# Column-form projections of a float32 encoder trunk: three 256-column products in one half of a bank in place of one 512-column and one 256-column product

## The chip, the cores and the metric

The kernel runs on one core of one Trainium2 chip. The metric is device time in microseconds of one execution; the number that counts is the median of several runs. Lower is better.

## What is computed

The program is a trunk of four post-norm encoder layers over 256 tokens of width 1024 in float32. Every layer is a token mixer followed by a SwiGLU feed-forward part, each with a residual and a layer norm:

```python
for i in range(DEPTH):                      # DEPTH = 4
    kind = i % 3                            # banded attention, GLA, differential attention, banded attention
    y = mixer(h)                            # x @ w_qkv (or w_in) ... @ w_o
    h = layer_norm(DN_ALPHA * h + y)
    h = layer_norm(DN_ALPHA * h + (silu(h @ w_gate) * (h @ w_up)) @ w_down)   # hidden width 2816
```

Nearly all arithmetic lies in the projections: 256 tokens against weight matrices with 1024 or 2816 rows.

## The kernel before

**Two-part float32 products.** TensorE is fed float32r operands. Each float32 operand is split into a high part and a low part, and a product a·w is the sum of three partial products: high·high, high·low and low·high. Activations lie transposed in SBUF as an operand of eight k-tiles `[128, 512]`: columns 0 to 255 are the high parts of the 256 tokens, columns 256 to 511 their low parts. Weights come by DMA on SP's queue in pieces of two k-tiles by 512 columns (`w_tiles`, L99 to L117); ScalarE makes the high part (L110), VectorE the low part (L111).

**Two forms of a projection.** `run_rows` (L141 to L180) puts 128 tokens on the output partitions and 512 weight columns in a bank of PSUM. Its three products, L175, L176 and L177, each load 128 columns of the activations into the array as the stationary operand and stream 512 weight columns. L175 and L176 use the same stationary tile `xh`.

`run_cols` (L182 to L204) puts 128 weight columns on the output partitions and streams the tokens. It works through a chunk of 512 weight columns: four blocks in the order 0, 2, 1, 3, each with eight k-tiles. For one k-tile (a "step" below) L196 streams all 512 columns of the operand, high and low, against the high weights into a whole bank; L197 streams the 256 high columns against the low weights into the first half of the bank. So the bank holds two halves that have to be added, and that is what the `done` callbacks do: ScalarE copies the second half to SBUF and VectorE adds the first half to it.

**Where the column form is used.** The query and key projections of the three attention layers (`qk_done`: four chunks each, L384 to L396), the queries of the GLA layer (`q_done`: one chunk, L729 and L730), and the gate and up projections of the feed-forward part from the third chunk on (`col_done`: nine chunks in each of four layers, L868 to L875). That is 3·4 + 1 + 4·9 = 49 chunks, 49·4·8 = 1568 steps. In the feed-forward part blocks 0 and 1 are gates (Silu, L871), and blocks 2 and 3 are multiplied by them and split into the high and low parts of the hidden operand (`put`, L211 and L212).

**Order of the work.** Each engine runs its instructions in program order. The order is written out by hand: `defer` puts a mixer's follow-up work off by a number of half-steps, and `tick`, called after every second k-tile in the column form, lets it in between the products. PSUM has four banks for projections (`mm`) and four for everything else (`tp`).

**Other products that the prediction uses.** `gate1` of the GLA layer (L667) runs eight products of 256 columns in a row, each with its own 128x128 float32r stationary tile, all into the same 256 columns of one bank. `values2` (L512 to L514) runs three products of 512 columns and then three of 256 columns; L513 and L514 use the same stationary tile `vh`.

Of the kernel before, what the change touches and what calls it, by code (L numbers as in the profile page):

```python
# [12 lines left out]
ALU = mybir.AluOpType  # L13
# [12 lines left out]
RAWB = 6  # weight loads under way, 2 k-tiles each  # L26
WB = 8  # split weights on chip, 2 k-tiles each
LAG = 10  # k-tiles that token half 1 runs behind half 0
# Half-steps of the tensor engine (see run_rows) by which work is put off.
# [6 lines left out]
def trunk_kernel(  # L36
# [63 lines left out]
    # ---------------------------------------------------------------- weights  # L100
    def w_tiles(chunk, s, fine=False):
        """Loads the k-tiles 2s, 2s+1 of a 512-column chunk of the weights and
        returns, per k-tile, their float32r parts (high, low)."""
        raw = wp.tile([P, 2, 512], F32, tag="raw", bufs=RAWB, name=nm("raw"))
        wh = wp.tile([P, 2, 512], F32R, tag="wh", bufs=WB, name=nm("wh"))
        wl = wp.tile([P, 2, 512], F32R, tag="wl", bufs=WB, name=nm("wl"))
        src = chunk[s].rearrange("p (k n) -> p k n", k=2)
        for k in (slice(0, 1), slice(1, 2)) if fine else (slice(0, 2),):
            nc.sync.dma_start(raw[:, k, :], src[:, k, :])
            nc.scalar.copy(out=wh[:, k, :], in_=raw[:, k, :])  # L110
            nc.vector.tensor_tensor(  # L111
                out=wl[:, k, :],
                in0=raw[:, k, :],
                in1=wh[:, k, :].bitcast(F32),
                op=ALU.subtract,
            )
        return [(wh[:, k, :], wl[:, k, :]) for k in range(2)]  # L117

    def late_load(dst, src, seen):
        """A load that is needed late, held back until `seen` is written, to  # L120
        leave the DMA queues to the weights."""
        nc.gpsimd.tensor_copy(dst[:, 0:1], seen)
        nc.gpsimd.dma_start(dst, src)

    # Work of the mixers that follows from a finished product is put off by a
    # number of half-steps (one k-tile of 512 columns for one token half), so
    # that the tensor engine has products to run while its inputs are made.
# [13 lines left out]
    def run_rows(chunks, lag=LAG, order=None, fine=0):  # L141
        """Products in row form (tokens on partitions, 512 columns a bank).
        chunks: (weights, k-tiles, src, done); src(kt) gives the high | low
        k-tile of all tokens, done(t, bank) reads the finished product.
        order lists (token half, chunk, k-tile); without it token half 1 runs
        lag k-tiles behind half 0."""
# [35 lines left out]
    def run_cols(w, src, done):  # L182
        """Products in column form: 128 columns of the weights on partitions,
        all 256 tokens in the free dimension. The bank of a column block holds
        the product with the tokens' high parts | with their low parts (high
        weights only), to be added up."""
        wt = []
        for s in range(NKT // 2):
            wt += w_tiles(w, s)
        for blk in (0, 2, 1, 3):  # L190
            b = bank("mm")
            cs = slice(blk * P, (blk + 1) * P)
            for kt in range(NKT):
                wh, wl = wt[kt]
                xk = src(kt)
                nc.tensor.matmul(b, wh[:, cs], xk, start=kt == 0, stop=False)  # L196
                nc.tensor.matmul(  # L197
                    b[:, :256], wl[:, cs], xk[:, :256], start=False, stop=kt == NKT - 1
                )
                if kt == NKT - 1:  # L200
                    done(blk, b)
                if kt % 2:
                    tick(1)
# [3 lines left out]
    # ------------------------------------------------------------- transposes  # L207
    def put(dst, ks, cs, val):
        """Writes val as the high and low parts of k-tiles ks, tokens cs."""
        h = dst[:, ks, cs]  # L210
        nc.scalar.copy(out=h, in_=val)  # L211
        nc.vector.tensor_tensor(  # L212
            out=dst[:, ks, slice(256 + cs.start, 256 + cs.stop)],
            in0=val,
            in1=h.bitcast(F32),
            op=ALU.subtract,
        )

    def split_T(src_cols, dst, t, k0, n):
        """Transposes n [128,128] blocks (row form in src_cols) into the k-tiles  # L220
        k0.. of token half t of dst."""
        b = bank()
        for k in range(n):
            nc.tensor.transpose(  # L224
                b[:, k * P : (k + 1) * P], src_cols[:, k * P : (k + 1) * P], ident
            )
        put(
            dst,
            slice(k0, k0 + n),
            slice(t * P, (t + 1) * P),  # L230
            b[:, : n * P].rearrange("p (k c) -> p k c", k=n),
        )

    def operand():
        """High | low parts of 8 k-tiles of all tokens."""
        return slab([P, NKT, 4 * P], F32R)
# [4 lines left out]
    # ------------------------------------------------------------- layer norm  # L241
# [12 lines left out]
    class Norm:  # L254
# [12 lines left out]
        def load(self, seen):  # L267
            """The next of the loads that the norm waits for."""
# [63 lines left out]
    def out_proj(OT, w, norm):  # L332
        """The k-tiles that need the last of the mixer's output come late, and
        enough of half 1 after half 0 to cover the norm of half 0."""
# [10 lines left out]
    # ------------------------------------------------- banded softmax attention  # L345
    def attention(xT, wqkv, bias_ap, w_o, norm, diff, src=None, **first):
        """One column block of 128 holds two 64-wide score maps: two heads, or
        the two maps of one differential head."""
# [30 lines left out]
        def qk_done(g):  # L379
            qk = qk_all[:, g, :, :]  # L380

            def done(blk, b):
                lo = k1([P, 256])
                if blk < 2:  # L384
                    nc.scalar.mul(lo, b[:, 256:], 0.125)
                    nc.vector.scalar_tensor_tensor(
                        out=qk[:, blk, :],
                        in0=b[:, :256],
                        scalar=0.125,
                        in1=lo,  # L390
                        op0=ALU.mult,
                        op1=ALU.add,
                    )
                    return
                nc.scalar.copy(out=lo, in_=b[:, 256:])
                nc.vector.tensor_tensor(  # L396
                    out=qk[:, blk, :], in0=b[:, :256], in1=lo, op=ALU.add
                )
# [83 lines left out]
        def turn2(c, pr):  # L482
            """Key block 0: half 0 of both heads, half 1 of both; key block 1:
            half 1 of both heads."""
# [17 lines left out]
        def values2(c, ph, pl):  # L502
            """Values of both heads against the weights of each: the rows of
            the other head are not read."""
# [101 lines left out]
    # ------------------------------------------------- gated linear attention  # L606
    def gla(xT, norm):
# [21 lines left out]
        # Low-rank gate: the columns 0..15 of the stationary tile are the high  # L629
        # parts of w_g1 and 32..47 the low parts (what follows them, the next  # L630
        # k-tile's, gives rows that nothing reads); w_g2 stands in the same
        # rows, so that the second product adds both up, and its bias in row 64.
# [94 lines left out]
        def q_done(blk, b):  # L727
            lo = k1([P, 256])
            nc.scalar.mul(lo, b[:, 256:], HK ** -0.5)  # L729
            nc.vector.scalar_tensor_tensor(  # L730
                out=qT[:, blk, :],
                in0=b[:, :256],
                scalar=HK ** -0.5,
                in1=lo,
                op0=ALU.mult,
                op1=ALU.add,
            )
# [104 lines left out]
    # ----------------------------------------------------------------- swiglu  # L842
    def ffn(xT, layer, norm):
# [19 lines left out]
        def col_done(c):  # L863
            g = {}

            def done(blk, b):
                lo = k1([P, 256])
                nc.scalar.copy(out=lo, in_=b[:, 256:])  # L868
                nc.vector.tensor_tensor(out=lo, in0=b[:, :256], in1=lo, op=ALU.add)  # L869
                if blk < 2:  # L870
                    nc.scalar.activation(lo, lo, AF.Silu)  # L871
# [3 lines left out]
                nc.vector.tensor_tensor(out=lo, in0=lo, in1=gg, op=ALU.mult)  # L875
# [19 lines left out]
    # ------------------------------------------------------------------ trunk  # L895
# [36 lines left out]
def _layouts(inputs):  # L932
    """Weights laid out chunk by chunk as the kernel reads them, x also with
    its tokens last, and the relative-position tables laid out per (query
    partition p, key column c): the key sits c - 128 - p places after the query."""
# [4 lines left out]
    def tiles(w, pairs=0):  # L940
        """[L, K, N] to [L, chunk, K / 256, 128, 2 * 512]; the first `pairs`
        chunks hold 256 columns of each of the first two parts of that width."""
# [68 lines left out]
```

## Time and profile before

| | |
|---|---|
| median of 3 runs | 1212.04 us (1210.23 to 1212.31) |
| span of the profiled execution, first to last instruction | 1209.5 us |
| mean granted TensorE clock, share of full speed | 0.998 |
| instructions | 17080 |
| TensorE matmuls / weight loads | 6224 / 6224 |
| VectorE / ScalarE busy | 829.6 us / 665.5 us |

The profiled execution has no time beside its span; the span is 2.5 us below the median of the runs. The page of the profile lists a matmul's time from its start to the modelled end of its pipeline, so the durations of neighbouring matmuls overlap; the pace of TensorE is read from the distance of their starts. "PEld" is the weight load, which overlaps the matmuls.

### The profile page before, as it was taken

To read this page: it belongs to the slowest core of one execution; us is meant where nothing else is said; L and a number is where in the kernel's file an instruction comes from. 1 tells how busy PE (TensorE), PEld (TensorE's weight loads), DVE (VectorE), ACT (ScalarE), POOL (GpSimd) and SP (SyncE) were. 2 spreads that over 40 slices of the span, in tenths; PEclk is the share of its full clock that TensorE was granted. 3 is DMA by queue.
4 is the path that set the end of the run, shared out by engine and by line. 5 is a ranking of instruction groups with operands and counts; after the bars stand their busy time and mean duration, and the time that the engine had idled before them with its cause. 6 is when DMAs were issued, how large, how long until landed. Compare 5 with 4: busy or idle time off the path is not lost.

```text
span 1209.5 us, 17080 instructions
## 1 busy us (share of the span) xinstructions
PE 1191.5 (99%) x6224; PEld 993.6 (82%) x6224; DVE 829.6 (69%) x1418; ACT 665.5 (55%) x1169; POOL 97.7 (8%) x188
## 2 busy tenths in 40 slices
PE   7999999999999999999999999999999999999997
PEld 5888888888887888888887778888888888888885
DVE  6687866745656777764667787676466888666644
ACT  6566555643664455663446656556344774665531
POOL 0130000000101000000012110000001200000000
PEclk9999999999999999999999999999999999999999
DMA  9654646556464456555564355665557544655641
GB/s 340 225 189 140 210 173 226 175 176 194 155 229 136 137 195 230 193 184 187 189 226 152 122 168 188 225 198 171 188 185 235 188 126 156 205 208 197 205 143 35
DMA packets 62772, 223.88 MB, mean 185 GB/s; under 512 B 7264, under 2 KB 7776, under 8 KB 62688
## 3 DMA queue, kind: packets, MB, share of 16 engines
q1 hardware_dynamic: 58176, 207.64, 52.1%
q0 software_dynamic: 4512, 15.14, 3.5%
q8 instruction: 49, 0.80, 0.3%
q14 instruction: 35, 0.29, 0.1%
HBM read 221.71 MB, written 1.05 MB: 184 GB/s over the span
## 4 chain that ended last, share of the span: by engine, by line
PE 94%; DVE 2%; ACT 2%; DMA 1%; POOL 0%; issue 0%; SPq 0%; POOLq 0%; DVEq 0%; ACTq 0%
PE mm L196 28%; PE mm L175 15%; PE mm L176 15%; PE mm L197 15%; PE mm L177 15%; PE tp L422 2%; PE tp L224 2%; ACT k L445 1%; PE tp L491 1%; DVE k L430 1%; DMA raw<-in_a_qkv_dram 1%; DVE wl L111 0%; PE tp L512 0%; PE tp L514 0%; PE tp L513 0%
## 5 line engine op out<-in xcount | busy, mean ns | idle before, releaser
L111 DVE TENSOR_TENSOR wl<-raw,wh 128x1024 fp32r<-128x1024 f32 (+1 forms) x394 | 476.0, 1214 | 180.6 <-ACT wh L110 177.7
L196 PE MATMUL mm<-slab,wh 128*128 128x512 f32 x1568 | 555.6, 397 | 0.0
L110 ACT CAST wh<-raw 128x1024 fp32r<-128x1024 f32 (+1 forms) x394 | 406.4, 1047 | 196.7 <-PE mm L177 185.2
L197 PE MATMUL mm<-slab,wl 128*128 128x256 f32 x1568 | 440.8, 281 | 0.0
L196 PEld LDWEIGHTS mm<-slab,wh 128*128 128x128 f32 x1568 | 294.3, 188 | 71.1 <-issue 4.6
L175 PE MATMUL mm<-wl,slab 128*128 128x512 f32 x784 | 311.5, 397 | 7.9 <-DVE wl L111 7.9
L177 PE MATMUL mm<-wh,slab 128*128 128x512 f32 x784 | 307.4, 392 | 0.0
L176 PE MATMUL mm<-wh,slab 128*128 128x512 f32 x784 | 307.2, 392 | 0.0
L197 PEld LDWEIGHTS mm<-slab,wl 128*128 128x128 f32 x1568 | 296.5, 189 | 0.7 <-issue 0.3
L175 PEld LDWEIGHTS mm<-wl,slab 128*128 128x128 f32 x784 | 147.8, 189 | 41.1 <-DVE wl L111 8.5
L177 PEld LDWEIGHTS mm<-wh,slab 128*128 128x128 f32 x784 | 147.6, 188 | 31.7 <-DVE slab L212 0.8
L176 PEld LDWEIGHTS mm<-wh,slab 128*128 128x128 f32 x784 | 147.8, 189 | 30.4 <-issue 1.8
L869 DVE TENSOR_TENSOR k<-mm,k 128x256 f32<-128x256 f32 x144 | 60.6, 421 | 82.9 <-ACT k L868 82.9
L868 ACT COPY k<-mm 128x256 f32<-128x256 f32 x144 | 53.7, 373 | 71.4 <-PE mm L197 71.1
L871 ACT ACTIVATE k<-k 128x256 f32<-128x256 f32 x72 | 29.8, 414 | 46.7 <-DVE k L869 46.7
L245 POOL TENSOR_SCALAR sm<-mv 128x1 f32<-128x1 f32 x16 | 14.1, 883 | 500.4 <-DVE mv L300 500.4
L211 ACT CAST slab<-k 128x256 fp32r<-128x256 f32 (+1 forms) x76 | 31.8, 418 | 40.9 <-DVE k L875 37.4
L212 DVE TENSOR_TENSOR slab<-k,slab 128x256 fp32r<-128x256 f32 (+1 forms) x76 | 33.0, 435 | 23.1 <-ACT slab L211 23.1
L445 ACT ACTIVATE k<-k,nmx 128x128 f32<-128x128 f32 x96 | 42.5, 444 | 8.4 <-DVE nmx L441 8.3
L211 ACT CAST slab<-tp 128x512 fp32r<-128x512 f32 (+1 forms) x56 | 27.1, 495 | 26.6 <-PE tp L224 24.5
L430 DVE CUSTOM_DVE_ANT_0 k<-tp,k 128x128 f32<-128x128 f32 x96 | 28.6, 353 | 10.1 <-PE tp L422 9.0
L212 DVE TENSOR_TENSOR slab<-tp,slab 128x512 fp32r<-128x512 f32 (+1 forms) x56 | 30.6, 569 | 4.6 <-ACT slab L211 4.5
(133 smaller groups left out, 669.5 us busy)
## 6 DMA issues: line engine op xcount, KB each, us to landing
raw<-in_w_gu_dram SPq DMA_DIRECT2D x176, 512.0 KB, 4.4
raw<-in_w_down_dram SPq DMA_DIRECT2D x88, 512.0 KB, 4.2
raw<-in_a_qkv_dram SPq DMA_DIRECT2D x46, 512.0 KB, 4.7
raw<-in_b_in_dram SPq DMA_DIRECT2D x24, 512.0 KB, 3.6
raw<-in_c_qkv_dram SPq DMA_DIRECT2D x24, 512.0 KB, 3.6
raw<-in_a_o_dram SPq DMA_DIRECT2D x16, 512.0 KB, 3.9
k<-in_a_bias_dram POOLq DMA_DIRECT2D x16, 256.0 KB, 4.5
lng<-in_ln_g_dram POOLq DMA_DIRECT2D x8, 512.0 KB, 5.7
```

Source lines behind the costliest of these rows:

```text
L110: nc.scalar.copy(out=wh[:, k, :], in_=raw[:, k, :])
L111: nc.vector.tensor_tensor(out=wl[:, k, :], in0=raw[:, k, :], in1=wh[:, k, :].bitcast(F32), op=ALU.subtract,)
L175: nc.tensor.matmul(b, xh, wl, start=first, stop=False)
L176: nc.tensor.matmul(b, xh, wh, start=False, stop=False)
L177: nc.tensor.matmul(b, xl, wh, start=False, stop=last)
L196: nc.tensor.matmul(b, wh[:, cs], xk, start=kt == 0, stop=False)
L197: nc.tensor.matmul(b[:, :256], wl[:, cs], xk[:, :256], start=False, stop=kt == NKT - 1)
L211: nc.scalar.copy(out=h, in_=val)
L212: nc.vector.tensor_tensor(out=dst[:, ks, slice(256 + cs.start, 256 + cs.stop)], in0=val, in1=h.bitcast(F32), op=ALU.subtract,)
L445: nc.scalar.activation(pr[:, m, SL[t]], pr[:, m, SL[t]], AF.Exp, bias=nmx[:, t, m : m + 1], accum_out=sm[:, t, m : m + 1],)
L868: nc.scalar.copy(out=lo, in_=b[:, 256:])
L869: nc.vector.tensor_tensor(out=lo, in0=b[:, :256], in1=lo, op=ALU.add)
```

## The change

In `run_cols` the one 512-column product against the high weights becomes two of 256 columns, one for the high and one for the low parts of the tokens, and all three products are added up in the same 256 columns of the bank. The `done` callbacks receive that half bank as the finished product: the copy of the second half and the addition are gone. The other lines of the diff only take comments and docstrings out.

```diff
             for kt in range(NKT):
                 wh, wl = wt[kt]
                 xk = src(kt)
-                nc.tensor.matmul(b, wh[:, cs], xk, start=kt == 0, stop=False)
-                nc.tensor.matmul(
-                    b[:, :256], wl[:, cs], xk[:, :256], start=False, stop=kt == NKT - 1
-                )
+                o, xh, xl = b[:, :256], xk[:, :256], xk[:, 256:]
+                nc.tensor.matmul(o, wh[:, cs], xh, start=kt == 0, stop=False)
+                nc.tensor.matmul(o, wh[:, cs], xl, start=False, stop=False)
+                nc.tensor.matmul(o, wl[:, cs], xh, start=False, stop=kt == NKT - 1)
                 if kt == NKT - 1:
-                    done(blk, b)
+                    done(blk, o)
...
         def qk_done(g):
             def done(blk, b):
-                lo = k1([P, 256])
                 if blk < 2:
-                    nc.scalar.mul(lo, b[:, 256:], 0.125)
-                    nc.vector.scalar_tensor_tensor(
-                        out=qk[:, blk, :],
-                        in0=b[:, :256],
-                        scalar=0.125,
-                        in1=lo,
-                        op0=ALU.mult,
-                        op1=ALU.add,
-                    )
+                    nc.scalar.mul(qk[:, blk, :], b, 0.125)
                     return
-                nc.scalar.copy(out=lo, in_=b[:, 256:])
-                nc.vector.tensor_tensor(
-                    out=qk[:, blk, :], in0=b[:, :256], in1=lo, op=ALU.add
-                )
+                nc.scalar.copy(out=qk[:, blk, :], in_=b)
...
         def q_done(blk, b):
-            lo = k1([P, 256])
-            nc.scalar.mul(lo, b[:, 256:], HK ** -0.5)
-            nc.vector.scalar_tensor_tensor(
-                out=qT[:, blk, :],
-                in0=b[:, :256],
-                scalar=HK ** -0.5,
-                in1=lo,
-                op0=ALU.mult,
-                op1=ALU.add,
-            )
+            nc.scalar.mul(qT[:, blk, :], b, HK ** -0.5)
...
         def col_done(c):
             def done(blk, b):
                 lo = k1([P, 256])
-                nc.scalar.copy(out=lo, in_=b[:, 256:])
-                nc.vector.tensor_tensor(out=lo, in0=b[:, :256], in1=lo, op=ALU.add)
                 if blk < 2:
-                    nc.scalar.activation(lo, lo, AF.Silu)
+                    nc.scalar.activation(lo, b, AF.Silu)
                     g[blk] = lo
                     return
                 gg = g.pop(blk - 2)
-                nc.vector.tensor_tensor(out=lo, in0=lo, in1=gg, op=ALU.mult)
+                nc.vector.tensor_tensor(out=lo, in0=b, in1=gg, op=ALU.mult)
```

## Rows read from the trace of the kernel before

**Rows 1.** The page, part 1: busy us (share of the span) xinstructions of each engine.

```profile
span 1209.5 us, 17080 instructions
...
PE 1191.5 (99%) x6224; PEld 993.6 (82%) x6224; DVE 829.6 (69%) x1418; ACT 665.5 (55%) x1169; POOL 97.7 (8%) x188
```

**Rows 2.** The page, part 4: the chain that ended last, by engine.

```profile
PE 94%; DVE 2%; ACT 2%; DMA 1%; POOL 0%; issue 0%; SPq 0%; POOLq 0%; DVEq 0%; ACTq 0%
```

**Rows 3.** Waits of the matmuls: us in total, times, longest us.

```profile
PE mm L175 <- DVE wl L111: 7.9, 2, 6.5
PE tp L578 <- DVE k L565: 0.7, 1, 0.7
PE tp L533 <- DVE k L465: 0.3, 1, 0.3
```

**Rows 4.** Window, column stage of the first feed-forward part: busy us (instructions), clock, DMA.

```profile
core 0: us, PE busy (x) PEld busy (x) DVE busy (x) ACT busy (x) POOL busy (x), PEclk, DMA share, GB/s
150.00:248.00 98.00, 98.00 (x557) 85.05 (x556) 64.79 (x102) 57.88 (x103) 3.83 (x7) 1.00 0.56 193
```

**Rows 5.** Line L196 in all four such stages: ns min/median/max, first and last start us.

```profile
L196 PE MATMUL mm<-slab,wh x279: 395/398/403, 149.7 to 247.9; 128*128 128x512 f32 x140
L196 PE MATMUL mm<-slab,wh x280: 391/391/391, 444.8 to 541.5; 128*128 128x512 f32 x140
L196 PE MATMUL mm<-slab,wh x281: 395/398/403, 743.6 to 842.5; 128*128 128x512 f32 x141
L196 PE MATMUL mm<-slab,wh x281: 391/391/396, 1043.6 to 1140.7; 128*128 128x512 f32 x141
```

**Rows 6.** Matmuls of a column stage, five steps: start us, us, engine, line, operation.

```profile
500.11 0.28 PE L197 MATMUL mm<-slab,wl 128*128 128x256 f32 x1
500.23 0.39 PE L196 MATMUL mm<-slab,wh 128*128 128x512 f32 x1
...
501.96 0.39 PE L196 MATMUL mm<-slab,wh 128*128 128x512 f32 x1
```

**Rows 7.** Timeline of matmuls, a row stage (17 starts apart).

```profile
299.99 0.39 PE L175 MATMUL mm<-wl,slab 128*128 128x512 f32 x1
...
303.84 0.39 PE L177 MATMUL mm<-wh,slab 128*128 128x512 f32 x1
```

**Rows 8.** Timeline of matmuls around the gate's eight products.

```profile
310.50 1.10 PE L667 MATMUL tp<-slab,k 128*128 128x256 f32 x8
311.44 0.40 PE L175 MATMUL mm<-wl,slab 128*128 128x512 f32 x1
```

**Rows 9.** Timeline of weight loads around the gate's eight products.

```profile
310.28 1.11 PEld L667 LDWEIGHTS tp<-slab,k 128*128 128x128 f32 x8
```

**Rows 10.** Timeline: the values' three 256-column products and their successor.

```profile
108.28 0.28 PE L512 MATMUL tp<-k,slab 128*128 128x256 f32 x1
...
108.64 0.40 PE L175 MATMUL mm<-wl,slab 128*128 128x512 f32 x1
```

**Rows 11.** Groups by line, weight loads: count, busy us, mean ns, idle before.

```profile
L196 PEld LDWEIGHTS mm<-slab,wh 128*128 128x128 f32 x1568 | 294.3, 188 | 71.1 <-issue 4.6
...
L513 PEld LDWEIGHTS tp<-k,slab 128*128 128x128 f32 x32 | 6.0, 188 | 0.9
L514 PEld LDWEIGHTS tp<-k,slab 128*128 128x128 f32 x32 | 6.0, 188 | 0.8
```

**Rows 12.** The page, part 5: groups of the fold and what follows it.

```profile
L869 DVE TENSOR_TENSOR k<-mm,k 128x256 f32<-128x256 f32 x144 | 60.6, 421 | 82.9 <-ACT k L868 82.9
L868 ACT COPY k<-mm 128x256 f32<-128x256 f32 x144 | 53.7, 373 | 71.4 <-PE mm L197 71.1
L871 ACT ACTIVATE k<-k 128x256 f32<-128x256 f32 x72 | 29.8, 414 | 46.7 <-DVE k L869 46.7
```

**Rows 13.** A line of the other folds: ns min/median/max, first and last start us.

```profile
L386 DVE SCALAR_TENSOR_TENSOR slab<-mm,k x24: 415/417/425, 35.4 to 986.5; 128x256 f32<-128x256 f32 x24
```

**Rows 14.** Lines that stand in for the new reads of PSUM.

```profile
L855 ACT ACTIVATE k<-mm x16: 384/384/386, 128.5 to 1041.2; 128x256 f32<-128x256 f32 x16
```

## Prediction

> **What bounds the kernel now.** I read the page first. TensorE has a matmul under way for 99% of the span, VectorE for 69%, ScalarE for 55% [rows 1]. A busy matmul row alone proves little, since the listed durations overlap, so the next two views matter more. The chain that ended last runs through TensorE for 94% of its length, through VectorE and ScalarE for 2% each [rows 2]. And the list of waits shows what TensorE waited for: 7.9 + 0.7 + 0.3 = 8.9 us in all, of which 6.5 us is one wait for the first weights [rows 3]. So outside the start about 2.4 us of the span belong to matmuls that waited for another engine. The reader is to see from this that the kernel is a stream of matmuls at the full granted clock, and that work taken off ScalarE and VectorE has next to no wait to shorten.
>
> What counts is the pace of that stream in the column form. It is read from the distance of starts, not from the 398 or 280 ns that the listing gives one matmul. In the four feed-forward stages line L196 starts 279, 280, 281 and 281 times [rows 5], which gives per step 98.2/278 = 353, 96.7/279 = 347, 98.9/280 = 353 and 97.1/280 = 347 ns: two levels, mean **350 ns**. They hold 4·9·4·8 = 1152 of the 1568 steps; I use 350 for the others too. Inside a step the 512-column product takes some 230 ns to the next start and the 256-column product 120 (with five steps in 1.73 us, 346 each [rows 6]). In the row form every product has 512 columns and a new stationary tile, and 17 starts take 3.85 us, 226.5 ns each [rows 7].
>
> **The change part by part.**
>
> *The added matmul and weight load.* The streamed columns of a step stay 768: 512 + 256 before, three times 256 after. The number of matmuls and of weight loads goes from two to three. It could be hoped that the second product with the high weights needs no load, as it has the stationary tile of the first. The trace says otherwise: L513 and L514 share their stationary tile and each shows 32 loads [rows 11]. So 1568 matmuls and 1568 loads are added, and the step becomes three times the pace of a 256-column product that brings its own load.
>
> That pace is the whole question, and the trace has no long run of such products, only short ones. The nearest is the gate: eight products, own tile each, same 256 columns of a bank, from 310.50 to the next start at 311.44, so 0.94/8 = 117.5 ns [rows 8]. Its eight loads take 1.11 us from first start to last end [rows 9]; less the last load's 0.19 and the 0.23 that the second load waited for the first of the eight products, six distances remain in 0.69 us, 115 ns. In the column form a 256-column product is followed after 110 to 120 ns [rows 6]. The three of the values take 108.28 to 108.64, 120 each [rows 10]. Lower end: half of a settled 512-column product, 226.5/2 = 113, since the same columns cannot stream faster. Upper end: 120. I take **117**, by the gate, which is the longest run and has the pattern nearest to the new one (its moving operand comes in two pieces of 128 columns, the only difference that I see).
>
> The sum: 3·117 = 351 against 350, +1 ns on 1568 steps, **+1.6 us**. With 113 it is 3·113 = 339, -11 ns, -17 us; with 120 it is 360, +10 ns, +15.7 us. Each ns in the pace of the 256-column product is 3·1568 = 4.7 us in the time. That leverage, not the gain on other engines, makes the range.
>
> The Trainium skill ("TensorE: Matmul & The Clock Gate", section "Back-to-back issue gap") gives an isolated matmul at full clock N/2.4 + 2.5 ns, which is 109 for 256 columns and 216 for 512. By it the step would go from 325 to 327.5 ns, an estimate of +3.9 us; the rows here are slower on both sides (226.5 and 117), so the sum goes by them.
>
> *The folds.* 144 copies of 373 ns on ScalarE and 144 additions of 421 ns on VectorE go in the feed-forward parts [rows 12]: 53.7 and 60.6 us. In attention and GLA 52 additions go, at 417 ns of L386's row [rows 13] 21.7 us, and the ScalarE instruction stays, writing the result itself. So VectorE falls from 829.6 to about 747 us, ScalarE from 665.5 to about 612. The gates' Silu reads PSUM now: L855 does that in 384 ns where L871 from SBUF takes 414 [rows 12, 14], so no loss. The up product is one VectorE multiplication out of PSUM, as the removed addition was, 421 ns. All of it lies beside the matmul stream: in the first feed-forward column stage VectorE is busy 64.79 of 98 us and ScalarE 57.88, TensorE all 98 [rows 4]. Value on the path: nothing there, and at most the 2.4 us of waits outside the start [rows 3]. Two of these three waits are on short VectorE chains of the differential attention that contain no fold; I take **-0.5 us**, ends 0 and -2.4.
>
> *Banks.* A column block takes 8·350 ns = 2.8 us and four banks rotate, so a bank has 8.4 us until it is wanted again. It was held through copy and addition, 0.8 us; now it is held through one read. For the up blocks that read waits for the gate, whose block ended one block earlier; Silu takes 0.4 us, well inside. No wait is added, nothing is queued behind a new one, and if this cover failed the price would be one visible bank wait per block, which the present kernel does not show at all [rows 3].
>
> *The rest.* DMA carries the same bytes at a share of 0.56 [rows 4]; no transfer is moved. The matmuls beside the column stages, the transposes between them, the start and the tail are unchanged.
>
> **Sum.** +1.6 - 0.5 = +1.1 us on a span of 1209.5, so 1210.6, and with the 2.5 us that the median of the runs stands above the span, **1213.1 us**, say 1213.0.
>
> **The rivals.**
>
> A. *Forecast: a run of 256-column products settles at 116.5 to 117.5 ns.* Steps of 349.5 to 352.5, -0.8 to +3.9 us, with the folds 1210.7 to 1215.4. For it: the gate. Against: eight products are a short run, and the column stages show that the stream can settle at either of two levels 6 ns apart [rows 5].
>
> B. *It settles slower, at 118 to 120 ns or a little above: the three tiles of the values show 120 [rows 10].* Then the weight load, which can start only about when the product before it starts, has become what sets the distance. From 117.6 on it decides against the change; at 118.5 it is 1220, at 120 +15.7 - 0.5 = 1227 us. Against it: the gate's eight do not show it.
>
> C. *It settles faster.* If the long product is what costs the odd 4 ns (230 in the column form against 226.5 in the row form [rows 6, 7]), a run of equal products may settle near half of the row form, 113 to 115 ns: at 113 1195 us, at 115 -8 - 0.5, 1204 us. For it: the row form, whose equal products run at the lowest pace seen. Against it: no group of 256-column products here is followed at 113.
>
> D. *The relief of VectorE and ScalarE tells after all,* by shorter follow-up chains in attention: at most the 2.4 us above, 1210 to 1211 with the forecast's step.
>
> E. *The loads become a plain bound.* If a load occupied its path for its listed 188 ns [rows 11], a step would take 3·188 = 564 ns and the kernel 1212 + 1568·0.214 = 1548 us. Against it: the present window has 556 loads in 98 us, 176 ns each [rows 4], and the gate 115 ns [rows 9], so listed loads overlap. The Trainium skill ("Perfetto Trace Analysis", section "Identifying the Most-Contended Engine") judges TensorE by the busy share of the weight loads rather than of the matmuls; by the sum of load times it would rise to 993.6 + 294.3 = 1288 us, above the whole span, and speak plainly against the change. The rows above show that this sum is no occupancy.
>
> F. *The shared tile is loaded once after all.* Then the middle product needs no load, and the step may near 3·113: 1195 us. Against it: [rows 11].
>
> **How the numbers follow.** I call a difference of 0.2%, 2.4 us, what a measurement of this kernel tells from no change: the band is 1209.6 to 1214.5. Chances: A 0.45, B 0.29, C 0.15, D 0.06, E and F together 0.05. Same gets most of A (0.37) and part of D (0.04): 0.41. Slower gets the upper edge of A (0.05), B and the milder forms of E (0.02): 0.36. Faster gets C, F and the remainders of A and D: 0.23. The likeliest case alone spans 1210 to 1216. The range for 8 in 10 takes in all of B up to 120 ns, 1227, with 1 us for the error of the reading, and of C the milder half down to 1203; what is left out is the far half of C with F, and E.
>
> **What would show it.** In the profile after: 1568 more matmuls and loads. The distance of starts in the feed-forward column stages gives the pace at once: three per step, 351 ns per step if A holds, 360 for B, 340 to 345 for C. Waits of matmuls should stay near 9 us with the same three lines; a bank wait would refute the part on banks. VectorE should show 747 us and ScalarE 612, with the share of TensorE in the chain unchanged; if the time falls while the step stays at 350 ns or more, the relief was worth more than I gave it. A row form that is no longer at 226.5 ns, or a clock below 1.00, would mean a cause that I have not listed.

## The result and the profile after

The changed kernel takes **1231.47 us** (median of 4 runs, 1230.90 to 1232.06) against 1212.17 us for the kernel before in the same runs: ratio 1.0162, 95% interval 1.0148 to 1.0177. It is slower by 19 us. The prediction was 1213.0 us, range 1203 to 1228, with 0.36 on slower; the time lies outside the range. The profiled execution has a span of 1230.4 us against 1209.5, so 20.9 us are to be found; that execution is the slowest of the four (1232.06 us, 1.7 above its span), one reason why the spans differ by more than the medians.

The page's first and fourth part, which answer to [rows 1, 2]:

```profile
PE 1209.5 (98%) x7792; PEld 1080.4 (88%) x7792; DVE 754.6 (61%) x1222; ACT 613.6 (50%) x1025; POOL 93.3 (8%) x188
...
PE 86%; ACT 6%; DVE 5%; issue 1%; POOL 1%; DMA 1%; SPq 0%; POOLq 0%; DVEq 0%; ACTq 0%
```

The counts came as foretold: 1568 matmuls and as many loads more. VectorE is busy 75 us less and ScalarE 52 (82 and 54 were foretold). But ScalarE and VectorE, with less to do, hold 11% of the chain in place of 4%, which was not foretold. Next the line of the first of the three products in the second, third and fourth feed-forward column stage, against [rows 5]; then matmuls and weight loads from the timeline of the first such stage, and its window, against [rows 4]:

```profile
L196 PE MATMUL mm<-slab,wh x278: 283/283/283, 451.9 to 551.6; 128*128 128x256 f32 x139
L196 PE MATMUL mm<-slab,wh x276: 283/283/283, 756.8 to 855.8; 128*128 128x256 f32 x138
L196 PE MATMUL mm<-slab,wh x276: 283/283/283, 1061.8 to 1160.8; 128*128 128x256 f32 x138
```

```profile
200.07 0.28 PE L196 MATMUL mm<-slab,wh 128*128 128x256 f32 x1
200.19 0.28 PE L197 MATMUL mm<-slab,wh 128*128 128x256 f32 x1
200.31 0.28 PE L198 MATMUL mm<-slab,wl 128*128 128x256 f32 x1
200.43 0.28 PE L196 MATMUL mm<-slab,wh 128*128 128x256 f32 x1
...
200.07 0.19 PEld L197 LDWEIGHTS mm<-slab,wh 128*128 128x128 f32 x1
200.19 0.19 PEld L198 LDWEIGHTS mm<-slab,wl 128*128 128x128 f32 x1
200.31 0.19 PEld L196 LDWEIGHTS mm<-slab,wh 128*128 128x128 f32 x1
```

```profile
155.00:254.00 99.00, 99.00 (x827) 99.00 (x827) 50.23 (x67) 45.23 (x68) 3.81 (x7) 1.00 0.56 190
```

The reader is to see three things. The step is 99.7/277 = 99.0/275 = **360 ns** in these stages (the first has the same length, 103.88 us): the two levels of before, 347 and 353, are gone. Every product follows at 120 ns, and the load of the next tile starts together with the product before it. And the row of weight loads, which had gaps before (85.05 of 98 us), has none: 99.00 of 99.00 us; the run with half a load, below, shows how little this says by itself. The clock is 1.00 in both.

Where the 20.9 us lie, each column stage taken from the start of its first column product to the start of the next row product (us):

| stage | before | after | difference |
|---|---|---|---|
| four feed-forward column stages | 101.96, 100.10, 101.96, 100.10 | 103.88, 103.89, 103.88, 103.89 | +11.4 |
| column stages of attention (layers 0, 2, 3) and GLA | 63.03, 63.20, 62.90, 11.29 | 65.91, 64.03, 65.66, 11.51 | +6.7 |
| row stages right behind the attention ones | 51.30, 52.09, 51.34 | 52.10, 52.37, 52.09 | +1.8 |
| first row stage and what stands ahead of it | 31.95 | 32.89 | +0.9 |
| all other row stages | | | 0.0 |

With 9.8 ns on each of 1568 steps the steps account for 15.4 us: all of the first line and 4.1 us of the second. Some 4.4 us are left in the attention layers, beside the steps. The 0.9 us at the start hardly belong to the change: "Products apart" below, which differs from the changed kernel only in the order of two products, has 31.77 us there.

### The profile page after: what moved, and what is told of

Read it like the earlier page. It is cut to its first block, busy times and chain, and to the rows that moved or that the text cites. A ratio compares the mean times of both kernels' runs of the same rounds, so it can differ in the third digit from the quotient of the medians.

```text
span 1230.4 us, 19879 instructions
## 1 busy us (share of the span) xinstructions
PE 1209.5 (98%) x7792; PEld 1080.4 (88%) x7792; DVE 754.6 (61%) x1222; ACT 613.6 (50%) x1025; POOL 93.3 (8%) x188
## 4 chain that ended last, share of the span: by engine, by line
PE 86%; ACT 6%; DVE 5%; issue 1%; POOL 1%; DMA 1%; SPq 0%; POOLq 0%; DVEq 0%; ACTq 0%
PE mm L175 14%; PE mm L176 14%; PE mm L177 14%; PE mm L196 13%; PE mm L198 13%; PE mm L197 13%; ACT k L432 3%; ACT wh L110 2%; DVE k L417 2%; DVE wl L111 2%; PE tp L223 1%; PE tp L409 1%; PE tp L478 1%; DMA raw<-in_a_qkv_dram 1%; DVE k L464 0%
## 5 line engine op out<-in xcount | busy, mean ns | idle before, releaser
L111 DVE TENSOR_TENSOR wl<-raw,wh 128x1024 fp32r<-128x1024 f32 (+1 forms) x394 | 472.5, 1214 | 271.4 <-ACT wh L110 269.6
L110 ACT CAST wh<-raw 128x1024 fp32r<-128x1024 f32 (+1 forms) x394 | 398.4, 1045 | 201.1 <-PE mm L177 183.4
L196 PE MATMUL mm<-slab,wh 128*128 128x256 f32 x1568 | 447.6, 285 | 0.0
L197 PE MATMUL mm<-slab,wh 128*128 128x256 f32 x1568 | 443.7, 283 | 0.0
L196 PEld LDWEIGHTS mm<-slab,wh 128*128 128x128 f32 x1568 | 300.9, 192 | 5.3 <-issue 5.0
L197 PEld LDWEIGHTS mm<-slab,wh 128*128 128x128 f32 x1568 | 300.7, 192 | 0.3
L198 PEld LDWEIGHTS mm<-slab,wl 128*128 128x128 f32 x1568 | 300.8, 192 | 0.0
L847 ACT ACTIVATE k<-mm 128x256 f32<-128x256 f32 x72 | 27.7, 385 | 105.6 <-PE mm L198 105.6
L851 DVE TENSOR_TENSOR k<-mm,k 128x256 f32<-128x256 f32 x72 | 30.3, 421 | 66.8 <-PE mm L198 66.8
```

The costliest lines, as they stand in the source:

```text
L111: nc.vector.tensor_tensor(out=wl[:, k, :], in0=raw[:, k, :], in1=wh[:, k, :].bitcast(F32), op=ALU.subtract,)
L196: nc.tensor.matmul(o, wh[:, cs], xh, start=kt == 0, stop=False)
L197: nc.tensor.matmul(o, wh[:, cs], xl, start=False, stop=False)
L198: nc.tensor.matmul(o, wl[:, cs], xh, start=False, stop=kt == NKT - 1)
```

## The experiments

All times beside one experiment are from the same chip as its runs of the kernel before.

**Split alone.** Folds as before; from the second k-tile of a block on the long product is two short ones, which stay in the two halves of the bank:

```diff
+                o, o2, xh, xl = b[:, :256], b[:, 256:], xk[:, :256], xk[:, 256:]
+                if kt == 0:
+                    nc.tensor.matmul(b, wh[:, cs], xk, start=True, stop=False)
+                else:
+                    nc.tensor.matmul(o, wh[:, cs], xh, start=False, stop=False)
+                    nc.tensor.matmul(o2, wh[:, cs], xl, start=False, stop=False)
```

> Before, with the 512-column product of the k-tiles 1 to 7 of every column block split into two of 256 columns, which stay in the two halves of the bank; the folds are kept. Theory (each product with its load costs its columns at 2.4 GHz plus 13.3 ns, whatever it adds to): steps of 360 ns in seven of eight k-tiles, 1152 of 1568 steps in the feed-forward part rise by 9.8 * 7/8, so 1212 + 13.5 = 1224 to 1227 us, with the waits of the attention layers as before. Rival (products that add into the same 256 columns right behind each other wait for PSUM): here two of the three follow on other columns, so steps near 350 ns and 1212 us. Rival (the folds being gone is what changed the rest): as the theory, but without the 4 us that the changed kernel loses beside its steps.

Measured: 1229.07 us against 1211.02, ratio 1.0143 (1.0124 to 1.0161). Its timeline:

```profile
200.06 0.28 PE L201 MATMUL mm<-slab,wh 128*128 128x256 f32 x1
...
201.15 0.28 PE L201 MATMUL mm<-slab,wh 128*128 128x256 f32 x1
```

Nine products in 1.09 us, 121 ns each in this stretch, although two of three neighbours write different columns; the four feed-forward column stages take 103.64 us each, against 103.88 in the changed kernel. Adding into the same columns is not the cause; the split by itself is most of the loss. The time is 2 us above my upper figure, and 1.6 us of that lie ahead of the first column product (33.59 us against 31.95). The attention and GLA column stages and the row stages right behind the attention ones grow by 5.5 us, of which the longer steps explain 3.8. So some 1.8 us of the 4.4 that the changed kernel loses there appear with the folds still in place.

**Products apart.** The changed kernel with the order high·high, low·high, high·low, so that the shared tile is not loaded twice running:

> The changed kernel with the three products in the order high*high, low*high, high*low, so that no two neighbours share a stationary tile. Theory (every load takes its 120 ns, shared or not): steps of 360 ns, 1231 us. Rival (loading the same tile twice in a row is what holds up): steps nearer 350 ns, 1216 us.

Measured once: 1230.87 us, feed-forward column stages of 103.88 us as in the changed kernel. That a tile is the same as the one before neither helps nor hurts here.

**Half a load.** The changed kernel; in six of eight k-tiles the stationary tile has 64 columns, and half of the output rows leave out these k-tiles:

```diff
+                n = 64 if 0 < kt < NKT - 1 else P
+                cw = slice(blk * P, blk * P + n)
...
+                q = b[:n, :256]
+                nc.tensor.matmul(q, wh[:, cw], xh, start=kt == 0, stop=False)
...
```

> The changed kernel with a stationary tile of 64 columns instead of 128 in the k-tiles 1 to 6 of every block, so that half of the output rows leave out these k-tiles. Theory (fixed 13.3 ns beside the columns streamed): distance of starts stays 120 ns, 1231 us. Rival (the load of 128 columns, 107 ns at 1.2 GHz and some start-up, sets the distance of 120 ns): the load takes half and the distance falls towards 107 to 113 ns in six of eight k-tiles, 7 to 13 ns on 7056 products but half of it hidden at changes, 1180 to 1205 us.

Measured once: 1213.65 us. Its timeline inside the short-load k-tiles, its loads grouped by shape, and a window of its first feed-forward column stage (columns as in [rows 4]):

```profile
200.43 0.28 PE L199 MATMUL mm<-slab,wh 128*64 128x256 f32 x1
...
201.45 0.28 PE L199 MATMUL mm<-slab,wh 128*64 128x256 f32 x1
```

```profile
L200 PEld LDWEIGHTS mm<-slab,wh 128*64 128x64 f32 x1176 | 157.7, 134 | 0.0
...
L201 PEld LDWEIGHTS mm<-slab,wl 128*128 128x128 f32 x392 | 75.2, 192 | 0.0
```

```profile
152.00:247.00 95.00, 95.00 (x826) 95.00 (x825) 50.98 (x68) 44.39 (x67) 3.82 (x7) 1.00 0.60 204
```

Nine products in 1.02 us: 113 ns, the half of a settled 512-column product that the prediction had as its lower end. The count of products and loads and the columns streamed are those of the changed kernel; the stationary tile has half the columns. With it both the load and the output rows are halved, and this run cannot part the two; the next run speaks for the load. The theory that I had on record, a fixed 13.3 ns per product whatever the load, is refuted. The rival had the likelier cause and too large a gain: the distance went down to 113 ns and no further. The window shows one thing more: the row of loads is full here too, 95.00 of 95.00 us, although the stages (99.83 us) are shorter than those of the changed kernel by 4 us. A row of loads without gaps does not by itself mean that the loads set the pace.

**Half a stream.** The changed kernel; in six of eight k-tiles the third product streams 128 tokens and leaves out that partial product for the other 128:

```diff
+                n = 128 if 0 < kt < NKT - 1 else 256
+                nc.tensor.matmul(
+                    b[:, :n], wl[:, cs], xk[:, :n], start=False, stop=kt == NKT - 1
+                )
```

> The changed kernel; in the k-tiles 1 to 6 of every block the third product streams 128 instead of 256 columns, so half of the tokens leave out that partial product there. Theory (the load of 128 columns sets the distance of 120 ns): the step stays at 360 ns although a sixth of its columns is gone, 1231 us. Rival (columns streamed plus a fixed 13.3 ns): 306.7 ns in six of eight k-tiles, 63 us less, 1168 us. Rival between (load 107 to 113 ns): steps of 347 to 353 ns, 1216 to 1223 us.

Measured once: 1234.1 us, above all three expectations. The differential attention's column stage alone was 72.89 us, 8.9 above the changed kernel's; the transposes waited 5.0 us for VectorE there (L523 for L455), and the granted clock was 0.93 in this stage. So the steps are read where nothing else interferes. The feed-forward stages took 101.46 us. Timeline of matmuls, then of loads:

```profile
200.73 0.34 PE L197 MATMUL mm<-slab,wh 128*128 128x256 f32 x1
200.90 0.28 PE L198 MATMUL mm<-slab,wh 128*128 128x256 f32 x1
201.02 0.22 PE L199 MATMUL mm<-slab,wl 128*128 128x128 f32 x1
201.08 0.33 PE L197 MATMUL mm<-slab,wh 128*128 128x256 f32 x1
...
201.78 0.34 PE L197 MATMUL mm<-slab,wh 128*128 128x256 f32 x1
...
200.67 0.19 PEld L197 LDWEIGHTS mm<-slab,wh 128*128 128x128 f32 x1
200.78 0.19 PEld L198 LDWEIGHTS mm<-slab,wh 128*128 128x128 f32 x1
...
202.07 0.19 PEld L197 LDWEIGHTS mm<-slab,wh 128*128 128x128 f32 x1
```

A sixth of the columns is gone, yet a step takes (201.78 - 200.73)/3 = 350 ns, where the stream alone would need 113 + 113 + 57 = 283. The short product is followed after 60 ns, but the next one then takes 170. The loads come at 200.67 to 202.07, twelve distances of 117 ns in the mean (single ones 108 to 124). In steps it is the rival in between of the three that I had listed: a sixth of the stream less wins 10 ns of the 77 that it would win if the stream set the step. So the stream does not set it. Of the two things that half a tile had halved, load and output rows, the load is then the likelier cause, since a cost of writing output rows should shrink with the columns streamed too; this is argued, not shown.

**Folds gone alone.** The callbacks of the changed kernel with the products of before; the low parts of the tokens are left out of the result:

> The changed callbacks with the products of before (512 + 256 columns); the low parts of the tokens are computed into the second half of the bank and left out of the result. Theory (steps alone set the stages; the rest of the loss, some 4 us, is that the planner now puts a split of weights on VectorE ahead of the negated maxima in 8 of 16 head pairs of the banded layers, 2 before): steps as before at 347 or 353 ns, and 1213 to 1217 us, with waits of the transposes for the scaled weights of softmax in the banded layers. Rival (less work on VectorE and ScalarE shortens the path): 1208 to 1211 us. Rival (the rest of the loss comes with the shorter products): 1212 us.

Measured: 1220.46 us against 1211.02, ratio 1.0071 (1.0053 to 1.0090). 196 VectorE instructions fewer, the same products, and 9 us more: worse than all three expectations. Two things happened. The second feed-forward stage now runs like this (line L196; before, [rows 5], 96.7/279 = 347 ns):

```profile
L196 PE MATMUL mm<-slab,wh x282: 395/398/477, 446.9 to 546.2; 128*128 128x512 f32 x141
```

99.3/281 = 353 ns, the slower of the two levels; so does the fourth, and both stages grow from 100.10 to 101.97 us, +3.7 in all. And the banded layers' column stages take 65.24 and 64.93 us instead of 63.03 and 62.90, the row stages behind them 0.9 more each, +6.0 together. The order written by hand is not the last word: the framework plans each engine's order anew, and with the folds out it interleaves transposes and products differently (in layer 0's column stage the transposes of softmax stand in nine groups between the products, six before) and puts a split of weights (`wl`, L111) ahead of the negated maxima of softmax in 8 of 24 head groups, against 2 before. The waits that I had expected of these transposes hardly appear: 0.3 us in the view of waits.

**Negated maxima first.** That order was tested in the changed kernel: every split of weights is queued behind the negated maxima that stand before it in the program:

```diff
+            if behind:
+                tc.add_manual_dep(low.ins, behind[-1], ...)
...
-            nc.vector.tensor_scalar_mul(nmx, mx, -1.0)
+            neg = nc.vector.tensor_scalar_mul(nmx, mx, -1.0)
+            behind.append(neg.ins.name)
```

> The changed kernel, with every split of weights on VectorE queued behind the negated maxima that stand before it in the program. Theory (a 1.2 us split ahead of them costs the attention stages 0.8 us each, about four to six times): 1226 to 1229 us, steps unchanged at 360 ns. Rival (the rest of the loss comes from the products): 1231.5 us.

and the same for the column stages of the banded layers alone:

> The changed kernel; in the column stages of the two banded layers alone, splits of weights on VectorE are queued behind the negated maxima that stand before them in the program. Theory (the split ahead of them delays softmax and so the transposes): the two column stages shrink from 65.9 and 65.7 to about 64.2 us each, the stage behind each by up to 0.7, nothing else moves: 1227 to 1229.5 us. Rival (the order costs nothing by itself, the wait only moves elsewhere): 1231 to 1232 us.

Measured: 1233.68 us (ratio 1.0180, 1.0158 to 1.0202) and 1233.62 us (1.0177, 1.0156 to 1.0197), both slower than the kernel before and neither faster than the changed kernel (1.0162, 1.0148 to 1.0177, run on another occasion); both theories missed. Here is what the order does in the changed kernel (timeline of VectorE in layer 0, then the transposes on TensorE, and last such transposes in the kernel before):

```profile
69.65 1.22 DVE L111 TENSOR_TENSOR wl<-raw,wh 128x1024 fp32r<-128x1024 f32 x1
70.78 0.17 DVE L428 TENSOR_SCALAR nmx<-mx 128x4 f32<-128x4 f32 x1
...
73.15 1.01 DVE L464 TENSOR_SCALAR k<-k,rec 128x128 f32<-128x128 f32 x4
...
73.00 0.28 PE L198 MATMUL mm<-slab,wl 128*128 128x256 f32 x1
73.58 1.18 PE L478 MATMUL tp<-ident,k 128*128 128x128 f32 x6 [0.30 <-DVE k L464]
74.52 0.36 PE L196 MATMUL mm<-slab,wh 128*128 128x256 f32 x1
```

```profile
54.09 0.81 PE L491 MATMUL tp<-ident,k 128*128 128x128 f32 x6
54.66 0.47 PE L196 MATMUL mm<-slab,wh 128*128 128x512 f32 x1
```

The split takes 1.22 us ahead of the 0.17 us that softmax needs, and TensorE stands before the transposes: 0.58 us from the last product to the first of them, then 0.94 us for six that take 0.57 without a wait. In the column stage of layer 0 this happens three times at 0.8 us in the changed kernel, and once at 0.45 us in the kernel before: some 2 of the 2.9 us that this stage loses, the rest being the longer steps. With all maxima first those three are gone, one of 0.6 us comes in at the start, and the column stage shrinks from 65.91 to 64.11 us, which the longer steps alone explain (63.03 + 128·0.0098 = 64.3). But the splits come later, and what waits for them pays, as the waits of the matmuls show, after (first two lines) and with all maxima first:

```profile
PE mm L175 <- DVE wl L111: 7.7, 2, 6.7
PE tp L478 <- DVE k L464: 2.4, 7, 0.5
```

```profile
PE mm L185 <- DVE wl L112: 11.0, 5, 6.7
PE tp L531 <- DVE k L463: 2.4, 3, 1.1
```

The wait of products for low weights rises from 7.7 to 11.0 us, and the differential layer's column stage from 64.03 to 66.87. With the banded layers alone the differential stage stays at 64.03, one of the three delays remains in layer 0 and the column stages take 65.00 and 65.61 us, but the row stages behind them grow from 52.1 to 53.6 and 53.7. So a split ahead of the maxima does cost softmax 0.8 us each time, and the place of that cost is shown; a gain from turning them round is not there, since the wait only moves. What the order costs by itself stays open, as the ties also make splits late.

**Regrouped pairs.** The kernel before with two long products, then two short ones:

```diff
+            for kt in range(0, NKT, 2):
+                for k in (kt, kt + 1):
+                    nc.tensor.matmul(b, wt[k][0][:, cs], src(k), start=k == 0, stop=False)
+                for k in (kt, kt + 1):
+                    nc.tensor.matmul(
+                        b[:, :256], wt[k][1][:, cs], src(k)[:, :256],
+                        start=False, stop=k == NKT - 1,
+                    )
...
```

> The kernel before, with the products of two k-tiles regrouped: two of 512 columns, then two of 256. The count of products and loads is that of before. Theory (a 256-column product costs at least the 120 ns that its load needs, a 512-column one 226.7 ns, and what a step of before takes beyond 346.7 ns is a conflict between load and stream at the change of lengths, which either settles at 353.3 or at nothing): half as many changes of length, steps of 347 to 350 ns in all four feed-forward parts, 1207 to 1212 us. Rival (every product after a change of length pays): two regrouped steps cost more than 2 * 353 ns, 1213 us or more.

Measured: **1208.44 us** against 1212.56, ratio 0.9966 (0.9954 to 0.9978): faster than both kernels. All four feed-forward column stages take 100.54 us, 349 ns per step, between the two levels of before, 347 and 353. That is 2.0 us less than the sum of the four before; the whole span is 2.5 us shorter. The medians differ by 4.1; the runs of before spread from 1210.0 to 1215.7, those of the pairs from 1208.3 to 1208.8, which I can't explain beyond the two levels.

**Groups of four and eight:**

> The kernel before, regrouped further: four products of 512 columns, then four of 256. Theory (a 256-column product costs 120 ns, the floor that its load sets, a 512-column one 226.7 ns, and the regrouped pairs, at 349.1 ns per step, lose 4.8 ns per two steps to the two changes of length): half as many changes again, steps near 348 ns, about 1.7 us less than the pairs: 1206 to 1208 us. Rival (the pairs merely happened on a good phase): steps of 350 to 353 ns, 1210 to 1214 us.

> The kernel before, with the eight products of 512 columns of a block first and then its eight of 256. Theory: steps near 347.3 ns, 2.8 us less than the pairs at the same order of the other work, 1205 to 1208 us; the transposes of attention move by up to half a block, which may cost some of it. Rival (a run of 256-column products pays 120 ns from the second product on, but the stream of 512 columns needs up to ten products to settle after it): steps of 349 to 353 ns, 1209 to 1214 us.

Measured: 1213.25 us (ratio 1.0000, 0.9991 to 1.0010) and 1210.73 us (0.9982, 0.9973 to 0.9991) against 1212.78; stages of 101.21 and 100.75 us, 351 and 350 ns per step. So fewer changes of length do not give shorter steps, and the theory behind this pair is refuted; `tick` moved as well, but these stages hold only two transposes, near their start, beside these products. Why pairs have the shortest sum stays open. The groups of eight show one thing that the prediction lacked, in their timeline:

```profile
200.49 1.11 PE L202 MATMUL mm<-slab,wl 128*128 128x256 f32 x8
201.44 2.00 PE L196 MATMUL mm<-slab,wh 128*128 128x512 f32 x8
```

Eight short products, own loads, 0.95/8 = 119 ns, against the gate's 117.5 with nearly the same pattern. By its single starts this run of eight goes 113, 119 and then six times 120 ns: the first product behind a long one is followed sooner, and the pace is 120 from the third on.

## Why the prediction was wrong

*What bounds the kernel:* right for the feed-forward and row stages, where the stream of matmuls set the end, and work taken off ScalarE and VectorE shortened nothing. In the attention layers it is not the whole story: TensorE's share of the chain fell from 94% to 86%, where the prediction had it unchanged.

*The added matmul and load:* here the step failed. "I take 117, by the gate, which is the longest run", and the pace is 120; the term of +1.6 us is 15.4. The mechanism was named (three loads for two, no load saved by the shared tile, 4.7 us for each ns of the pace), and rival B had place and price right: at 120 it gave +15.7 us on the steps. What misled was to take a run of eight for a settled one. The gate's eight distances are, by their single starts, 113, 118, 114, 119, 117, 116, 116 and 119 ns; their mean holds the early 113 behind the long product and no stretch at one pace. Why the later ones stay below the 120 of the groups of eight is open: the prediction named a difference, the moving operand in two pieces, and no run tests it. The values' 120 [rows 10] told the settled pace, and I set them aside.

It is tempting to add to the gate what the row products behind it lose, which would bring it to 120 as well. These lines of the kernel before follow [rows 8]; below them stand row products behind a settled run at 120, from the changed kernel:

```profile
311.67 0.40 PE L176 MATMUL mm<-wh,slab 128*128 128x512 f32 x1
...
312.60 0.39 PE L177 MATMUL mm<-wh,slab 128*128 128x512 f32 x1
```

```profile
254.67 0.28 PE L198 MATMUL mm<-slab,wl 128*128 128x256 f32 x1
254.79 0.40 PE L175 MATMUL mm<-wl,slab 128*128 128x512 f32 x1
...
255.95 0.39 PE L177 MATMUL mm<-wh,slab 128*128 128x512 f32 x1
```

From 311.44 to 312.60 and from 254.79 to 255.95 five row products take 1.16 us, where 1.13 are usual. The 0.03 us are the same behind eight short products and behind hundreds, so they belong to the return to long products and not to the pace of the short ones.

*Why it is 120.* Rival B's condition holds as far as the experiments go: with half a stationary tile 113, with the same tile apart 120, with other PSUM columns 120 to 121, with a stream cut by a sixth still 117 per load. So the size of the loaded tile sets the pace above 113 ns, and the stream has little to do with it. How a load comes to 120 ns is not shown. It is not the least distance of two loads, as the timeline of weight loads of the kernel before shows (six for transposes, then those of the products behind them):

```profile
53.98 0.69 PEld L491 LDWEIGHTS tp<-ident,k 128*128 128x128 f32 x6
54.64 0.19 PEld L196 LDWEIGHTS mm<-slab,wh 128*128 128x128 f32 x1
54.75 0.19 PEld L197 LDWEIGHTS mm<-slab,wl 128*128 128x128 f32 x1
```

The six loads of the transposes, listed at 140 ns each, follow each other at (0.69 - 0.14)/5 = 110 ns, and the second load for the products behind them comes 0.11 us after the first. That is less than the 113 ns of half a settled 512-column product, so neither a load nor a stream alone makes 120; that they wait for each other is argued, not shown.

*Rival E and the page behind it.* I put the loads as a plain bound at 188 ns each, 564 ns per step, and the step is 360. The Trainium skill ("Perfetto Trace Analysis", section "Identifying the Most-Contended Engine") judges TensorE's headroom by the share of peak arithmetic reached and by the busy share of the weight loads, the sum of their times over the window. Here that sum is 556·188 ns = 104.5 us in the 98 us before and 827·192 ns = 158.8 us in the 99 us after: it rises as the kernel gets slower, but it stands above the window in both. My 1288 us was no such sum either: 993.6 and 294.3 us are times with a load under way, overlaps counted once [rows 1, 11], and that time after the change is 1080.4 us. Nor does this second measure tell a bound, since the run with half a load has 95.00 of 95.00 us as well.

*The folds:* "-0.5 us, ends 0 and -2.4" had the wrong sign. Taken out by themselves they cost 9 us with the old products, since under the planner's new order the banded layers take 6.0 us more and the stream settles on its slower level in two feed-forward parts (+3.7). In the changed kernel, where the second of these does not occur, the remainder beside the steps is some 4.4 us in the attention layers, of which some 1.8 also appear with the folds kept. The term failed at its premise that work beside the stream can only be a gain when it goes. That the order moved is shown; which part of it is decisive is not, since mending one place only moved the wait.

*Banks:* right, no wait for a bank appears. *The row form, clock, DMA:* right, all row stages that do not follow attention are unchanged to 0.1 us, the one at the start aside.

*The range* took in B up to 120 ns, but with the folds' term at -0.5 and not at +4, so it ended 3.5 us short. The pace at 120 alone, with the folds as foretold, would have given 1226.9 us, inside the range; it took both errors to leave it.

## What to carry to other kernels

Before a long product is cut into short ones with their own weight loads, price the short one by a run with loads of the same size that is long enough to settle; the columns streamed do not give the price. In a short run read the single distances of starts, not their mean, since the first of them still belongs to what came before. A row of loads without gaps is no proof that the loads set the pace: halve the load, and then the stream, and see which one moves the time. And where a planner orders the instructions, a change that only removes work off the path is a new order as well; give it a term of either sign.

## What the runs showed of the hardware that was not expected

A stream of 512- and 256-column products in turn can settle at two levels for a whole stage, 347 or 353 ns per step, with the same instructions; in pairs it took 349 in all four stages. A product can start 60 ns after its load has started (the load of 200.67 and the product of 200.73 above), where 120 ns are usual, and the time is then lost in that product. The trace lists a load of 128 columns as 187 to 192 ns for the products and as 140 for the transposes, one of 64 columns as 134; none of these is the distance at which loads follow each other: 120 ns in a settled run of 256-column products, 113 with 64 columns, 110 in the transposes.
